# Twenty-four modulation vectors of layer 0 on the matrix engine, with the condition stationary and the weights moving

## The chip, the cores and the metric

The kernel runs on one core of one Trainium2 chip. TensorE (PE) multiplies matrices into eight PSUM banks, VectorE (DVE), ScalarE (ACT) and GpSimd (POOL) work on tiles in SBUF, and SyncE (SP) issues the DMAs. Each engine takes its instructions in a fixed order. The metric is the device time of one launch, in microseconds (us); the median of the runs counts.

## The reference, cut to what matters

One step of a hybrid diffusion backbone: two layers, 1024 latent and 128 context tokens, width 1024. Each layer begins with a modulation: from the condition `c` (and `c_ctx` for the context tokens) come six vectors of length 1024, which shift, scale and gate the stream.

```
mod = (jax.nn.silu(cvec) @ lp['w_mod'] + lp['b_mod'])[:, None, :]
sh1, sc1, g1, sh2, sc2, g2 = jnp.split(mod, 6, axis=-1)
h = x * (1 + sc1) + sh1
... = jnp.split(h @ lp['w_in'] + lp['b_in'], offsets, axis=-1)
mix = jnp.concatenate([a_out, m_out, g_out], axis=-1) @ lp['w_out']
x = layernorm(ALPHA * x + g1 * mix, lp['ln1_g'], lp['ln1_b'])
h2 = x * (1 + sc2) + sh2
```

`a_out` is latent attention, `m_out` an mLSTM, `g_out` an HGRN2 recurrence; they share the input projection. A SwiGLU feed-forward block follows, gated by `g2`.

## The kernel before

Per layer there are four phases: A (input projection, HGRN2, mLSTM, preparation of the attention's inputs), B (attention), C and D (output projection and feed-forward). Most products are made in three passes of reduced float32 (`mm3`, lines 155 to 157): each operand is split into a high and a low part, cast on ScalarE (L145, L150) and subtracted on POOL or DVE (L146, L151). `hhi` and `hlo` hold the two parts of the modulated stream. The HGRN2 and mLSTM products are plain float32.

The six modulation vectors of a layer are kept as 48 pieces of 128 values, `modfm[:, l, j, s]`, with j the piece and s one of the two conditions. Here "vector" means such a piece. In layer 0 pieces 0 to 15 are made in `start`, 16 to 23 in the background of the first projections, 24 to 39 in the background of the mLSTM, and 40 to 47 later. A background vector is a `mod_gemv`: one DMA of 128x1024 weights (L211), and for each of the two conditions one DVE instruction that multiplies the weights by the broadcast condition `cB` and sums along the row (L213). `mod_bias` (L220) adds the bias for eight at a time, and `gsave` (L225) writes the gate vectors to memory. Layer 1 makes none of its vectors in phase A; they are made in phase D of layer 0.

`start_mod` gives a generator. Each evacuation of the projection `gi` (L399) and of the attention's inputs takes one step of it, and each of the nine mLSTM blocks two.

Phase A in the order of the program, with the lines named later:

- `gi` projection (216 `mm3` products of 256 columns, evacuated by L399 on DVE), `prep`, and the projections for the attention
- HGRN2 for the first pair of heads: `states` (transposes L566, products L571), `outs` (products L601; POOL L614 to L617, ScalarE L618, DVE L619 to L623), with the projections of the second pair among them
- `ml_gates` (transposes L694, L741), then HGRN2 for the second pair, with `ml_states` (L781 to L807) and other projections among them
- `mlstm` for nine blocks: a broadcast load (L825), a mask on POOL (L832), exponentials on ScalarE (L835), products L830, L845 and L850 on PE, DVE L839 to L871, POOL L863 to L874
- `spill_gate` for `mo` and `gg`: 18 tiles of 24 `mm3` products with 256 columns, then DVE L336, ScalarE L337 (sigmoid or silu), POOL L338, and a store. In the program these come after `mlstm`.

Phase B begins with conversions of the attention's inputs. They are written into parts of `hhi` and `hlo`, which phase A's projections have read by then. The first score products and their maxima (L1134, L1135) lead to the first attention probabilities (L1183, L1184).

The PSUM banks are handed out from rings: `r_mm` is banks 0 to 2 (projections), `r_a` banks 3 and 4, `r_m` banks 5 to 7. A bank is written again only when its former content has been read, in the order of the program. Which ready instruction comes next on an engine is set when the program is built, by a list scheduler; an instruction whose inputs or whose bank aren't free yet is passed by later ones.

Of the kernel before, what the change touches and what calls it, by code (L numbers as in the profile page):

```python
# [15 lines left out]
BF16 = mybir.dt.bfloat16  # L16
AF = mybir.ActivationFunctionType
ALU = mybir.AluOpType
AX = mybir.AxisListType

P = 128
D = 1024
KD = 8
# [9 lines left out]
U = 1024  # L33
# [64 lines left out]
class Builder:  # L98
# [60 lines left out]
    def setup(self):  # L159
        nc, ctx, ins = self.nc, self.ctx, self.ins  # L160
# [3 lines left out]
        t = self.tile  # L164
# [5 lines left out]
        self.cols = t(self.pp, [P, DEPTH, NCOL], name="cols")  # L170
        nc.sync.dma_start(self.cols, ins["cols"])
        self.modfm = t(self.pp, [P, DEPTH, 48, 2], name="modfm")
        self.gates = t(self.pp, [P, NT, 16], name="gates")
        self.gT = t(self.pp, [16, P], name="gT")
        self.mhalf = t(self.pp, [P, 8], name="mhalf")
# [59 lines left out]
    def start(self, z):  # L235
        nc, ins = self.nc, self.ins
        accs = [(i // NB, i % NB, self.bank[i]) for i in range(7)]
        cin, cc = z([P, KD, 2]), z([P, KD, 2])
        cB, junk = [z([P, D]), z([P, D])], z([P, D], BF16)
        rm, rx, rt = z.ring(6, [P, U]), z.ring(6, [P, T]), z.ring(2, [P, T])  # L240
        nc.sync.dma_start(cin, ins["cvec"])
# [2 lines left out]
        xs, ws = [], []  # L244
# [35 lines left out]
        return ws, accs  # L280

    def start_mod(self, z, j0, j1):
        raw = z.ring(2, [P, U])
        cB, junk = [z([P, D]), z([P, D])], z([P, D], BF16)
        self.mod_init(cB)

        def gen():
            for j in range(j0, j1):
                self.mod_gemv(0, j, cB, raw.next(), junk)
                if j % 8 == 7:  # L290
                    self.mod_bias(0, j - 7, 8)
                if j == 23:
                    self.gsave(0, 16, self.r_m.next())
                yield

        return gen()
# [1393 lines left out]
def pack(i):  # L1690
# [7 lines left out]
    wm = f["w_mod"].reshape(DEPTH, KD, P, 48, P)  # L1698
    a["w_mod"] = np.concatenate([
        wm[0, :, :, :8].transpose(2, 3, 0, 1).reshape(8, P, 1024),  # L1700
        wm[0, :, :, 8:16].transpose(2, 1, 0, 3).reshape(8, P, 1024),
        wm[0, :, :, 16:].transpose(2, 3, 0, 1).reshape(32, P, 1024),
        wm[1].transpose(2, 3, 0, 1).reshape(48, P, 1024)], 0).reshape(DEPTH, 48, P, 1024)
    w = f["w_in"].reshape(DEPTH, KD, P, -1)
    units = np.zeros((DEPTH, 22, P, 1024), np.float32)
# [63 lines left out]
```

## Time and profile before

| | us |
|---|---|
| median of 3 runs | 3615.47 |
| lowest and highest | 3614.98, 3617.87 |
| the profiled execution | 3608.53 |
| its span | 3606.7 |
| PE busy | 3382.4 (94%) |
| DVE busy | 2251.9 (62%) |
| POOL busy | 1999.0 (55%) |
| ScalarE busy | 1635.2 (45%) |

The profiled execution is another one than the three timed runs. A row of the windows gives, for a stretch of time, how long each engine was busy in it and the clock that TensorE was granted (1.00 is 2.4 GHz, 0.50 is 1.2 GHz). A group by line gives the busy time of all instructions of one line, the mean of one, and how long the engine stood idle just before them and for whom. The timeline gives single instructions with their start; a matmul's duration overlaps the next one's start, so what one costs is read from start to start.

### The profile page before, as it was taken

The page shows a single profiled execution, that of the slowest core. Times are in us where ns is not written, and L with a number is a line of the kernel's source. Part 1 is how long each engine was busy: PE and PEld are TensorE (multiplying, and loading weights), DVE is VectorE, ACT ScalarE, POOL GpSimd, SP SyncE. Part 2 cuts the span into 40 slices and gives each one's busy share as a digit, 9 for nine tenths or more (in the row PEclk, how much of TensorE's full clock was granted, in tenths as well). Part 3 has the DMA queues.
Part 4 walks back from the last instruction along what each step waited for, and adds up shares of the span by engine and source line. Part 5 has one row for each costly group of instructions (what it writes and reads, how often), then busy time and mean ns, then how long its engine had stood idle before and what let it go on. Part 6 is the DMA issues. An engine that isn't in the chain of part 4 may idle for free. (4 is left out here: it accounts for less than half of the span.)

```text
span 3606.7 us, 56103 instructions
## 1 busy us (share of the span) xinstructions
PE 3382.4 (94%) x20556; PEld 3015.5 (84%) x20556; DVE 2251.9 (62%) x4487; ACT 1635.2 (45%) x2877; POOL 1999.0 (55%) x1750
## 2 busy tenths in 40 slices
PE   7998987998979999999889989989999899999989
PEld 7998876776779999988689888877767899999867
DVE  6878778556674444487776688765568544443344
ACT  4264654887343333312262646578863433333111
POOL 3465566877665555401454556457763555556345
PEclk9999976999989999999999999789999899999999
DMA  6211153002352222375422021401044322224232
GB/s 251 70 46 34 45 168 98 19 21 85 123 156 86 85 86 86 104 252 184 161 73 71 32 43 40 135 25 24 22 129 127 115 76 75 75 77 158 72 116 77
DMA packets 331274, 335.77 MB, mean 93 GB/s; under 512 B 191459, under 2 KB 270387, under 8 KB 330997
## 3 DMA queue, kind: packets, MB, share of 16 engines
q1 hardware_dynamic: 330996, 332.19, 29.3%
q8 instruction: 161, 2.64, 0.3%
q14 instruction: 117, 0.95, 0.1%
HBM read 263.54 MB, written 68.56 MB: 92 GB/s over the span
## 5 line engine op out<-in xcount | busy, mean ns | idle before, releaser
L151 POOL TENSOR_TENSOR t<-t,t 128x512 fp32r<-128x512 f32 (+3 forms) x318 | 440.5, 1387 | 384.9 <-ACT t L150 379.9
L1447 PE MATMUL bank<-hhi,t 128*128 128x256 f32 (+1 forms) x2816 | 571.2, 295 | 7.9 <-DVE t L1347 7.4
L150 ACT CAST t<-t 128x512 fp32r<-128x512 f32 (+5 forms) x404 | 270.5, 672 | 676.1 <-PE bank L1447 275.1
L155 PE MATMUL bank<-hhi,t 128*128 128x384 f32 (+1 forms) x1238 | 464.3, 381 | 24.8 <-ACT hhi L145 10.4
L157 PE MATMUL bank<-hhi,t 128*128 128x384 f32 (+1 forms) x1238 | 463.8, 376 | 5.8 <-DVE t L151 5.8
L156 PE MATMUL bank<-hlo,t 128*128 128x384 f32 (+1 forms) x1238 | 464.4, 375 | 4.6 <-POOL hlo L151 3.1
L1447 PEld LDWEIGHTS bank<-hhi,t 128*128 128x128 f32 x2816 | 456.4, 189 | 9.6 <-ACT t L150 7.4
L1185 POOL TENSOR_TENSOR t<-t,t 128x512 fp32r<-128x512 f32 (+1 forms) x304 | 384.2, 1283 | 123.4 <-ACT t L1184 107.4
L1447 PE MATMUL bank<-t,t 128*128 128x320 f32 (+1 forms) x3168 | 435.0, 297 | 4.6 <-ACT t L150 2.2
L1447 PEld LDWEIGHTS bank<-t,t 128*128 128x128 f32 x3168 | 428.2, 190 | 6.0 <-ACT t L150 3.0
L1447 PE MATMUL bank<-hlo,t 128*128 128x320 f32 (+1 forms) x1408 | 415.3, 295 | 0.1
L155 PE MATMUL bank<-t,hhi 128*128 128x256 f32 (+3 forms) x1232 | 387.1, 315 | 8.1 <-DVE t L1105 2.1
L156 PE MATMUL bank<-t,hhi 128*128 128x256 f32 (+3 forms) x1232 | 389.2, 316 | 4.9 <-POOL t L146 4.9
L157 PE MATMUL bank<-t,hlo 128*128 128x256 f32 (+3 forms) x1232 | 388.9, 316 | 0.1
L155 PEld LDWEIGHTS bank<-hhi,t 128*128 128x128 f32 x1238 | 241.4, 196 | 60.7 <-ACT hhi L145 11.3
L1135 DVE TENSOR_REDUCE t<-bank 128x1 f32<-128x384 f32 (+1 forms) x400 | 205.1, 539 | 129.9 <-PE bank L1134 127.5
L157 PEld LDWEIGHTS bank<-hhi,t 128*128 128x128 f32 x1238 | 240.9, 195 | 37.9 <-DVE t L151 9.0
L156 PEld LDWEIGHTS bank<-hlo,t 128*128 128x128 f32 x1238 | 241.3, 195 | 36.7 <-POOL hlo L151 3.9
L1447 PEld LDWEIGHTS bank<-hlo,t 128*128 128x128 f32 x1408 | 265.4, 189 | 0.4 <-issue 0.2
L213 DVE SCALAR_TENSOR_TENSOR t<-t,t 128x1024 bf16<-128x1024 f32 x176 | 239.4, 1360 | 36.0 <-DMA t<-in_w_mod_dram 29.0
L155 PEld LDWEIGHTS bank<-t,hhi 128*128 128x128 f32 x1232 | 240.4, 196 | 24.9 <-DVE t L1105 2.5
L156 PEld LDWEIGHTS bank<-t,hhi 128*128 128x128 f32 x1232 | 241.7, 196 | 21.1 <-POOL t L146 5.3
(355 smaller groups left out, 7250.6 us busy)
## 6 DMA issues: line engine op xcount, KB each, us to landing
t<-in_w_mod_dram SPq DMA_DIRECT2D x96, 512.0 KB
t<-in_w_ffn_in_dram SPq DMA_DIRECT2D x88, 512.0 KB
t<-in_w_ffn_out_dram SPq DMA_DIRECT2D x44, 512.0 KB
t<-in_w_in_dram SPq DMA_DIRECT2D x40, 512.0 KB
shid<-t SPq DMA_DIRECT2D x88, 160.0 KB
sx<-t SPq DMA_DIRECT2D x27, 512.0 KB
t<-sx SPq DMA_DIRECT2D x27, 512.0 KB
shid<-t SPq DMA_DIRECT2D x88, 128.0 KB
```

What stands on the lines that cost most here:

```text
L150: self.nc.scalar.copy(hi, src)
L151: (eng or self.nc.gpsimd).tensor_tensor(lo, src, hi.bitcast(F32), op=ALU.subtract)
L155: mm(ps, a[0], b[0], start=first, stop=False)
L156: mm(ps, a[0], b[1], start=False, stop=False)
L157: mm(ps, a[1], b[0], start=False, stop=last)
L213: nc.vector.scalar_tensor_tensor(junk, raw, 1.0, cB[s], op0=ALU.mult, op1=ALU.mult, accum_out=self.modfm[:, l, j, s:s + 1])
L1135: V.tensor_reduce(nm[:, i, b:b + 1] if i < 8 else nm[:, i, 3:4], ps, axis=AX.X, op=ALU.max, negate=True)
L1185: G.tensor_tensor(pl, e, ph.bitcast(F32), op=ALU.subtract)
L1447: mm(ps, a[x][:, k * P:(k + 1) * P], view(y, k, n0, n1), start=first and k == 0 and i == 0, stop=k == 3 and i == 2, skip_group_check=True)
```

## The change

`start_mod` makes four vectors at a time on PE. The weights of pieces 16 to 39 are laid out anew on the host, so that four loads hold 512 columns of the weight matrix for all 1024 rows. `cc`, the condition after silu, now stays in SBUF; it is the stationary operand with two columns. Eight plain float32 matmuls with 512 moving columns add up in one bank of `r_mm`, ScalarE copies the 2x512 result (L298 of the changed file), four small transposes turn it into columns (L301), and one DVE instruction adds the bias (L304). The broadcasts of the condition into `cB` for these vectors are gone, and so are 48 instructions of L213. A group takes three steps of the generator: one that issues the loads, an empty one, and one that computes.

```diff
--- before.py
+++ after.py
@@ -170,6 +170,7 @@
         self.cols = t(self.pp, [P, DEPTH, NCOL], name="cols")
         nc.sync.dma_start(self.cols, ins["cols"])
         self.modfm = t(self.pp, [P, DEPTH, 48, 2], name="modfm")
+        self.cc = t(self.pp, [P, KD, 2], name="cc")
         self.gates = t(self.pp, [P, NT, 16], name="gates")
         self.gT = t(self.pp, [16, P], name="gT")
         self.mhalf = t(self.pp, [P, 8], name="mhalf")
@@ -235,7 +236,7 @@
     def start(self, z):
         nc, ins = self.nc, self.ins
         accs = [(i // NB, i % NB, self.bank[i]) for i in range(7)]
-        cin, cc = z([P, KD, 2]), z([P, KD, 2])
+        cin, cc = z([P, KD, 2]), self.cc
         cB, junk = [z([P, D]), z([P, D])], z([P, D], BF16)
         rm, rx, rt = z.ring(6, [P, U]), z.ring(6, [P, T]), z.ring(2, [P, T])
         nc.sync.dma_start(cin, ins["cvec"])
@@ -280,16 +281,29 @@
         return ws, accs
 
     def start_mod(self, z, j0, j1):
-        raw = z.ring(2, [P, U])
-        cB, junk = [z([P, D]), z([P, D])], z([P, D], BF16)
-        self.mod_init(cB)
+        nc = self.nc
+        raw, row = z.ring(4, [P, U]), z.ring(1, [2, 512])
 
         def gen():
-            for j in range(j0, j1):
-                self.mod_gemv(0, j, cB, raw.next(), junk)
-                if j % 8 == 7:
-                    self.mod_bias(0, j - 7, 8)
-                if j == 23:
+            for j in range(j0, j1, 4):
+                ws = [raw.next() for _ in range(4)]
+                for u, w in enumerate(ws):
+                    nc.sync.dma_start(w, self.ins["w_mod"][0, j + u])
+                yield
+                yield
+                ps, r = self.r_mm.next(), row.next()
+                for k in range(KD):
+                    nc.tensor.matmul(ps[0:2, :], self.cc[:, k, :], ws[k // 2][:, (k % 2) * 512:(k % 2 + 1) * 512],
+                                     start=(k == 0), stop=(k == KD - 1))
+                nc.scalar.copy(r, ps[0:2, :])
+                ps = self.r_m.next()
+                for q in range(4):
+                    nc.tensor.transpose(ps[:, 2 * q:2 * q + 2], r[:, q * P:(q + 1) * P], self.ident[0:2, 0:2])
+                one = 1.0 if (j // 8) % 3 == 1 else 0.0
+                b = self.col(0, "bmod")[:, j:j + 4].unsqueeze(2).to_broadcast([P, 4, 2])
+                nc.vector.scalar_tensor_tensor(self.modfm[:, 0, j:j + 4, :], ps[:, 0:8].rearrange("p (j s) -> p j s", s=2), one, b,
+                                               op0=ALU.add, op1=ALU.add)
+                if j == 20:
                     self.gsave(0, 16, self.r_m.next())
                 yield
 
@@ -1699,7 +1713,8 @@
     a["w_mod"] = np.concatenate([
         wm[0, :, :, :8].transpose(2, 3, 0, 1).reshape(8, P, 1024),
         wm[0, :, :, 8:16].transpose(2, 1, 0, 3).reshape(8, P, 1024),
-        wm[0, :, :, 16:].transpose(2, 3, 0, 1).reshape(32, P, 1024),
+        wm[0, :, :, 16:40].reshape(4, 2, P, 6, 4, P).transpose(3, 0, 2, 1, 4, 5).reshape(24, P, 1024),
+        wm[0, :, :, 40:].transpose(2, 3, 0, 1).reshape(8, P, 1024),
         wm[1].transpose(2, 3, 0, 1).reshape(48, P, 1024)], 0).reshape(DEPTH, 48, P, 1024)
     w = f["w_in"].reshape(DEPTH, KD, P, -1)
     units = np.zeros((DEPTH, 22, P, 1024), np.float32)
```

The order of the instructions differs above all in four places. In the rows below `bank_63` to `bank_70` are banks 0 to 7; the changed file's lines are 14 higher than before from `start_mod` on.

TensorE, in the HGRN2 of the second pair of heads. Before (L601 and L571 are its products, L155 to L157 with 256 columns the spill's):

```order
L157 MATMUL bank_64<-t_134,hlo_77 128x256
L155 MATMUL bank_64<-t_134,hhi_76 128x256
L156 MATMUL bank_64<-t_138,hhi_76 128x256
L601 MATMUL bank_66<-t_1955,t_665 128x128
L571 MATMUL bank_70<-t_619,t_681 128x128 x2
L601 MATMUL bank_66<-t_1955,t_665 128x128
L601 MATMUL bank_67<-t_1955,t_665 128x128 x2
L601 MATMUL bank_66<-t_1955,t_665 128x128
L601 MATMUL bank_67<-t_1955,t_665 128x128
L571 MATMUL bank_69<-t_619,t_685 128x128 x2
L157 MATMUL bank_64<-t_134,hlo_77 128x256
L155 MATMUL bank_64<-t_134,hhi_76 128x256
```

After (L615, L585 and L580 are L601, L571 and L566 of before):

```order
L585 MATMUL bank_70<-t_615,t_681 128x128 x2
L580 MATMUL bank_68<-ident_71,t_623 128x128
L580 MATMUL bank_68<-ident_71,t_627 128x128
L580 MATMUL bank_70<-ident_71,t_623 128x128
L580 MATMUL bank_70<-ident_71,t_627 128x128
L585 MATMUL bank_69<-t_615,t_677 128x128 x2
L615 MATMUL bank_66<-t_665 128x128
L615 MATMUL bank_67<-t_665 128x128
L615 MATMUL bank_66<-t_665 128x128
L615 MATMUL bank_67<-t_665 128x128
L615 MATMUL bank_66<-t_665 128x128
L615 MATMUL bank_67<-t_665 128x128
```

The spill's products are gone from this place; 409 of them stood ahead of the first mLSTM product, and none does now.

TensorE, in the mLSTM. Before (L830, L845 and L850):

```order
L156 MATMUL bank_64<-t_138,hhi_76 128x256
L157 MATMUL bank_64<-t_134,hlo_77 128x256
L155 MATMUL bank_64<-t_134,hhi_76 128x256
L850 MATMUL bank_69<-t_611,t_4370 128x65
L845 MATMUL bank_70<-t_2986,t_4386 128x130 x2
L830 MATMUL bank_66<-t_4390,t_615 128x128 x2
L850 MATMUL bank_69<-t_611,t_4370 128x65 x3
L830 MATMUL bank_67<-t_4390,t_615 128x128 x2
L850 MATMUL bank_68<-t_611,t_4370 128x65 x4
L156 MATMUL bank_64<-t_138,hhi_76 128x256
```

After (L844, L859 and L864 are these lines; L296 is the new product):

```order
L859 MATMUL bank_69<-t_2991,t_4389 128x130 x2
L864 MATMUL bank_68<-t_607,t_4373 128x65 x3
L844 MATMUL bank_67<-t_4393,t_611 128x128 x2
L296 MATMUL bank_64<-t_4353,cc_81 2x512 x2
L864 MATMUL bank_70<-t_607,t_4373 128x65 x4
L296 MATMUL bank_64<-t_4357,cc_81 2x512
L864 MATMUL bank_69<-t_607,t_4377 128x65
L296 MATMUL bank_64<-t_4357,cc_81 2x512
L296 MATMUL bank_64<-t_4361,cc_81 2x512
L859 MATMUL bank_68<-t_2987,t_4393 128x130 x2
L864 MATMUL bank_69<-t_607,t_4377 128x65 x3
L296 MATMUL bank_64<-t_4361,cc_81 2x512
```

The new products stand among those of the first six blocks, 32 in all.

TensorE, at the last products of the mLSTM (L850, after the change L864). Before (L155 to L157 with 384 columns are phase B's first products):

```order
L845 MATMUL bank_68<-t_2986,t_4390 128x130 x2
L850 MATMUL bank_69<-t_611,t_4382 128x65 x4
L850 MATMUL bank_70<-t_611,t_4370 128x65 x4
L850 MATMUL bank_68<-t_611,t_4370 128x65 x4
L155 MATMUL bank_69<-hhi_76,t_5655 128x384
L156 MATMUL bank_69<-hlo_77,t_5655 128x384
L157 MATMUL bank_69<-hhi_76,t_5655 128x384
```

After:

```order
L155 MATMUL bank_63<-t_143,hhi_76 128x256
L156 MATMUL bank_63<-t_147,hhi_76 128x256
L864 MATMUL bank_68<-t_607,t_4373 128x65 x4
L157 MATMUL bank_63<-t_143,hlo_77 128x256
L155 MATMUL bank_63<-t_143,hhi_76 128x256
L156 MATMUL bank_63<-t_147,hhi_76 128x256
L157 MATMUL bank_63<-t_143,hlo_77 128x256
L155 MATMUL bank_64<-t_135,hhi_76 128x256
```

The products of phase B that followed here come later; in their place 388 of the spill's products stand in a row, and 44 among the mLSTM's last ones.

ScalarE, at the end of the spill. Before (L337 is the spill's, L835 the mLSTM's, L150 converts phase B's inputs):

```order
L337 ACT_TABLE_LOAD
L337 ACTIVATE t_162<-t_162 128x256
L150 CAST hhi_76<-t_5675 128x128
L835 ACT_TABLE_LOAD
L835 ACTIVATE t_4370<-t_4370,t_2802 128x128 x8
L150 CAST hhi_76<-t_5663 128x384
L150 CAST hhi_76<-t_5667 128x384
```

After (L351 is L337, L1059 is L1045 of before):

```order
L351 ACTIVATE t_163<-t_163 128x256
L351 ACTIVATE t_159<-t_159 128x256
L351 ACTIVATE t_163<-t_163 128x256
L1059 CAST t_5636<-t_5704 1x1152
L1059 CAST t_5728<-t_5704 1x1152
L1059 CAST hhi_76<-t_5704 1x1152
L150 CAST hhi_76<-t_5700 128x128
L150 CAST hhi_76<-t_5688 128x384
```

The conversions still stand behind the spill's last sigmoid, which now comes after the mLSTM's exponentials.

## Rows read from the trace of the kernel before

**Rows 1.** Page, part 1: engine, busy us, share of the span, instructions.

```profile
PE 3382.4 (94%) x20556; PEld 3015.5 (84%) x20556; DVE 2251.9 (62%) x4487; ACT 1635.2 (45%) x2877; POOL 1999.0 (55%) x1750
```

**Rows 2.** Windows: stretch, then PE, PEld, DVE, ACT, POOL busy; clock, DMA share, GB/s.

```profile
91.70:185.10 93.40, 88.08 (x702) 86.37 (x702) 80.99 (x245) 24.20 (x37) 46.08 (x46) 0.92 0.24 70
1900.80:1978.00 77.20, 77.20 (x674) 76.36 (x674) 46.59 (x192) 11.27 (x22) 29.47 (x33) 1.00 0.22 62
344.40:470.10 125.70, 120.07 (x929) 110.03 (x929) 94.77 (x249) 81.44 (x137) 75.38 (x111) 0.97 0.22 57
470.10:602.80 132.70, 95.58 (x429) 82.74 (x428) 117.61 (x321) 52.76 (x123) 93.97 (x94) 0.62 0.50 162
2143.60:2264.20 120.60, 115.10 (x907) 104.60 (x905) 98.45 (x256) 73.18 (x117) 75.59 (x106) 1.00 0.20 50
2264.20:2376.60 112.40, 94.92 (x450) 83.54 (x449) 90.92 (x287) 59.84 (x142) 55.22 (x65) 0.63 0.38 115
```

**Rows 3.** Lines L830, L1184 in layer 0: ns min/median/max, first to last start us.

```profile
L830 PE MATMUL bank<-t,t x72: 272/417/579, 470.1 to 533.3; 64*128 64x128 f32 x72
...
L1184 ACT CAST t<-t x152: 293/620/642, 602.8 to 914.5; 128x512 fp32r<-128x512 f32 x144, 128x128 fp32r<-128x128 f32 x8
```

**Rows 4.** Groups by line and form, DVE, 475 to 603 us: busy us, mean ns.

```profile
L213 DVE SCALAR_TENSOR_TENSOR t<-t,t 128x1024 bf16<-128x1024 f32 x32 | 42.7, 1334 | 1.8 <-DMA t<-in_w_mod_dram 1.8
L1135 DVE TENSOR_REDUCE t<-bank 128x1 f32<-128x384 f32 x19 | 9.6, 545 | 0.0
...
L213 DVE DVE_READ_ACCUMULATOR t<-t,t 128x1 f32 x32 | 2.5, 78 | 0.0
```

**Rows 5.** Timeline, PE, phase B: start us, us, line, operands, count.

```profile
653.91 0.40 PE L1181 MATMUL bank<-t,t 96*128 96x512 f32 x1
654.14 0.39 PE L1182 MATMUL bank<-t,t 97*128 97x512 f32 x1
```

**Rows 6.** Timeline, PE, first mLSTM products of layer 0.

```profile
476.35 0.71 PE L845 MATMUL bank<-t,t 128*128 128x130 f32 x4
476.99 0.71 PE L830 MATMUL bank<-t,t 64*128 64x128 f32 x4
477.63 0.88 PE L850 MATMUL bank<-t,t 128*128 128x65 f32 x6
478.44 0.71 PE L830 MATMUL bank<-t,t 64*128 64x128 f32 x4
```

**Rows 7.** Timeline, ScalarE and POOL, end of the spill in layer 0.

```profile
485.86 0.30 ACT L150 CAST hhi<-t 128x128 fp32r<-128x128 f32 x1
...
486.96 0.72 POOL L338 TENSOR_TENSOR t<-t,t 128x256 f32<-128x256 f32 x1
```

**Rows 8.** Windows of line L151 alone: DVE busy, POOL busy, clock, DMA.

```profile
487.00:603.00 116.00, 10.17 (x13) 21.46 (x16) 0.57 0.46 152
```

**Rows 9.** Timeline, PE, spill in layer 1: first and last of 38 rows.

```profile
2266.62 0.28 PE L156 MATMUL bank<-t,hhi 128*128 128x256 f32 x1
...
2270.81 0.28 PE L157 MATMUL bank<-t,hlo 128*128 128x256 f32 x1
```

**Rows 10.** Groups, DVE and POOL, 345 to 475 us: busy, mean ns, idle before.

```profile
L619 DVE TENSOR_TENSOR t<-t,t 128x192 f32<-128x192 f32 x18 | 7.9, 439 | 16.6 <-ACT t L618 16.6
L336 DVE TENSOR_TENSOR t<-bank,t 128x256 f32<-128x256 f32 x17 | 7.0, 413 | 3.5 <-DMA sgg<-t 3.5
...
L338 POOL TENSOR_TENSOR t<-t,t 128x256 f32<-128x256 f32 x17 | 12.6, 741 | 28.8 <-ACT t L337 28.1 <-DVE t L623 0.7
```

**Rows 11.** Timeline, PE, mLSTM of layer 1.

```profile
2284.75 1.97 PE L850 MATMUL bank<-t,t 128*128 128x65 f32 x8
2286.65 1.22 PE L830 MATMUL bank<-t,t 64*128 64x128 f32 x4
2287.80 0.69 PE L850 MATMUL bank<-t,t 128*128 128x65 f32 x2
```

**Rows 12.** Windows: 25 us of the mLSTM of layer 1.

```profile
2275.00:2300.00 25.00, 25.00 (x107) 22.72 (x107) 15.13 (x54) 22.55 (x58) 8.07 (x13) 0.50 0.57 180
```

## The prediction, made before the changed kernel was run

> **What bounds the kernel now.** I read the page first: TensorE (PE) is busy for 3382.4 us, 94% of the span [rows 1]. So the question is where PE is not the limit, and what the change does there. Next I cut the two layers' first phase into the same stretches and put them side by side [rows 2]. Layer 1 makes no modulation vectors in this phase, so it is a control for layer 0. Three stretches matter.
>
> Stretch A runs from the first evacuation of `gi` (L399) to the first state matmul (L571): 93.4 us in layer 0, 77.2 in layer 1 [rows 2]. In layer 1 PE is busy all the time; in layer 0 VectorE (DVE) also makes vectors 16 to 23 there. Stretch B runs from the last gate transposes (L741) to the first mLSTM product (L830): 125.7 us, PE busy 120.07. Stretch C runs from there to the first attention probabilities (L1184): 132.7 us, PE busy 95.58 at a granted clock of 0.62, DVE busy 117.61 [rows 2, 3]. C is the one stretch limited by DVE: vectors 24 to 39 cost it 32 x 1.334 = 42.7 us, and 2.5 us more for reading the accumulators [rows 4]. Layer 1 needs 112.4 us for C [rows 2]. So if the work simply vanished, the controls say some 16 us in A and 20 to 25 in B and C together (258.4 against 233.0).
>
> **What the change takes from DVE and puts on PE.** 48 of the products on DVE go, 48 x 1.334 = 64 us. In their place stand six groups of eight plain float32 matmuls with a 2-wide stationary operand and 512 moving columns. The trace counts two instructions for such a matmul, so 96. No row has a plain float32 matmul that wide. From below: reduced float32 with 512 columns starts every 0.233 us [rows 5]. From above: plain float32 with 130 columns and a full weight load starts every 0.16 us, (476.99 - 476.35) / 4, which scaled by columns is 0.63 [rows 6]. I take 0.43, the middle, since the narrow row also pays a load of 128 weight columns that a 2-wide operand doesn't need. A group then costs 16 x 0.43 = 6.9 us at full clock (3.7 to 10) and 13.8 at half. The Trainium skill, "FP8 and Floating Point Precision", TensorE Precision Notes, says that true FP32 takes four passes through the array; by it a matmul would take 4 x 512 / 2.4 GHz = 0.85 us as an estimate, and the six groups 41 us, the same sum; no run here shows the wide case. A 2x512 copy on ScalarE, four small transposes and one 128x8 add per group come to little on engines that are not the limit there.
>
> **Stretch A.** Two groups add 13.8 us to PE, and about 1 us for transposes and for the second group's weights, whose four loads wait for the first group. DVE loses 16 x 1.33 = 21 us. Layer 1 shows this stretch to be bound by PE as soon as DVE is free: 77.2 + 13.8 + 1 = 92, against 93.4. I take -1 us (-7 to +5, by the bounds of a group). DVE's relief is spent on PE's new work.
>
> **What moves: the spill matmuls.** This is the term that decides. The 432 matmuls of `spill_gate` (mo, gg; 128x256) come after `mlstm` in the program and use banks 0 to 2. Before, nothing in `mlstm` used these banks, so 409 of the 432 stand on PE ahead of the first L830, between the hgrn products. The new groups take banks from the same ring, so the spill now has to come after the last group: the order shows none of it in B, 44 among the last mLSTM products, and 388 in one piece behind the last one. And the conversions for phase B write into `hhi` and `hlo`, which the spill reads. Before, the spill's last gate product ran on POOL at 486.96 us and the first conversion on ScalarE at 485.86 [rows 7], so all of this conversion, 21.46 us of L151 on POOL and 10.17 on DVE [rows 8], lay beside the mLSTM. Now it starts when the 388 are done.
>
> Stretch B loses 409 x 0.113 = 46 us of PE work (38 rows, 2266.62 to 2270.81, so 0.113 each) [rows 9], but DVE then sets the pace: 94.77 us busy, less 7.0 for the spill's L336, gives 88. It waited 16.6 us there for ScalarE, and POOL 28.8 us in front of L338 [rows 2, 10]; both shrink when the spill's sigmoids no longer stand between the hgrn's steps. At 95% busy that is 93 us, at the 82% of layer 1's row (98.45 of 120.60) 107 [rows 2]. I take 100, the middle, a gain of 26.
>
> Stretch C falls into three pieces in a row. First the mLSTM with four groups. At full clock its own 72 + 64 + 144 instructions take 0.16, 0.16 and 0.135 us each [rows 6], 41 us; four groups 27.5; 44 spill matmuls 5: 73 in all. At half clock they take 0.29 and 0.24, (2287.80 - 2286.65) / 4 and (2286.65 - 2284.75) / 8 [rows 11], and with 0.29 for the 64 as well that is 74 us; groups 55, spill 5: 134. Which clock? In layer 1 PE is busy 25.00 of 25 us here at a clock of 0.50 [rows 12], so its own products don't raise it; the wide ones are unlike them. The weights also need time: 16 x 0.52 MB and 9 broadcasts of 0.52 MB are 13 MB, 81 us at the 162 GB/s of this stretch [rows 2], and the first loads of the weights stand behind four broadcasts. I take 95, between 73 and 134 and nearer to the first, since the wide products fill PE's columns as the spill's do. Second the 388 spill matmuls at 0.113 us: 44. Third the conversions and the first peaks: 21.5 on POOL [rows 8], then 19 reductions on DVE, 9.6 [rows 4], are 31 if all else hides under them; with an estimate of 8 for the casts ahead and the products between 39, and I take that (31 to 42). It was hidden under the mLSTM and the vectors before.
>
> The sum for B and C: 100 + 95 + 44 + 39 = 278, against 258.4, so +19.6; with A +19 us. From L1184 on the attention is bound by PE as before, and nothing is late that would absorb it. One load of weights is also moved up in SP's queue into the start, but a broadcast of the same size goes from there: nothing. The profiled execution took 3608.5 us (span 3606.7 and 1.8 around it), 7.0 below the median of 3615.5. So 3627 by that execution, and **3634.5 us** by the median.
>
> **Rival 1, faster.** The wide matmuls bring PE to full clock through the mLSTM and the weights arrive in time. Then 93 + 73 + 44 + 31 = 241, -17 us, with A -18: 3597. For it: the spill's products kept the clock at 0.97 in B [rows 2], and DVE has 45 us less to do. Against it: the serial order of mLSTM, spill and conversions remains, and with the likely B and third piece the first piece must stay under 75 us for any gain. The Trainium skill, "Perfetto Trace Analysis", Matmul Optimizations, says that the engine scales with utilization, so that matmuls should come back to back in batches; by that this rival would be the likely one, but the row of layer 1, back to back at half clock, disagrees [rows 12].
>
> **Rival 2, much slower.** PE stays at half clock through all four groups, or waits in them for weights, which in its queue also holds up the mLSTM products behind. Then 107 + 134 + 44 + 42 = 327, +69, with A +68: 3683. It decides once the first piece of C is over 115 us. The row of layer 1 speaks for it.
>
> **Rival 3, no change.** B is at 93 and the first piece near 82, and the gain in B pays for what is laid bare in C: within 7 us of 3615.5.
>
> **How the numbers follow.** My forecast, +8 to +40 us, has 0.42; rival 2 and all over +40, 0.20; rival 1, 0.22; rival 3, 0.16. Slower by over 0.2% (7 us, about what a measurement of this kernel can tell from none): 0.62; within: 0.16; faster: 0.22. The likeliest case alone spans 3623 to 3655. The range 3602 to 3670 leaves out the far half of rival 1 and the far end of rival 2, some 0.2 together.
>
> **What would show it.** Right: in the windows of the profile after, a stretch of some 44 us with nothing on PE but 128x256 matmuls at full clock after the last mLSTM product, DVE low in it, and the first `hhi` conversion right behind; B near 100 us; A within 5 us of 93. Wrong: 512-column matmuls far from 0.43 us at clock 1.00; a clock near 1.00 through the mLSTM (rival 1); PE waiting for `in_w_mod` there (rival 2); or spill matmuls that wait for something other than their bank. If B didn't shrink, the loss would be some 26 us larger.

## The result, and the profile after

The changed kernel takes 3639.11 us (median of 4 runs, 3631.05 to 3641.91) against 3615.22 for the kernel before on the same chip: 1.0064 times the time, 95% interval 1.0044 to 1.0085. It is slower by some 24 us. The profiled execution took 3640.93 us, with a span of 3639.1, 32.4 above that of before; the stretches below add up to this larger difference. In the code after, lines from L297 of before on are 14 higher: L399 is L413, L571 is L585, L830 is L844, L1184 is L1198.

The page of the kernel after, engines over the whole span, answers to [rows 1]:

```profile
PE 3430.1 (94%) x20676; PEld 3029.1 (83%) x20676; DVE 2190.2 (60%) x4394; ACT 1602.7 (44%) x2854; POOL 1972.0 (54%) x1750
```

DVE is relieved by 61.7 us, PE has 47.7 us more, and the share of PE is what it was. The page alone explains nothing; the stretches do. Windows of the kernel after (columns as in [rows 2]): stretch A, stretch B, the three pieces of C, and C as a whole.

```profile
86.10:188.40 102.30, 97.20 (x714) 84.24 (x713) 60.66 (x218) 25.33 (x40) 37.62 (x42) 0.97 0.24 69
...
350.60:460.60 110.00, 87.58 (x512) 76.41 (x512) 89.95 (x230) 37.76 (x93) 63.57 (x95) 0.70 0.17 40
460.60:543.80 83.20, 83.20 (x414) 50.11 (x414) 40.06 (x177) 19.49 (x59) 37.71 (x59) 0.89 0.51 167
543.80:592.00 48.20, 46.47 (x388) 46.26 (x386) 13.68 (x47) 11.30 (x23) 24.70 (x33) 1.00 0.29 89
592.00:640.40 48.40, 33.45 (x128) 28.77 (x129) 31.52 (x62) 30.95 (x63) 20.79 (x21) 0.64 0.33 102
460.60:640.40 179.80, 163.12 (x927) 125.14 (x927) 85.26 (x284) 61.73 (x144) 83.20 (x111) 0.85 0.40 129
```

Against [rows 2]: A is 8.9 us longer, but begins 5.6 earlier, so its end is 3.3 late. B is 15.7 us shorter, C 47.1 longer. The fourth row is the serial run of the spill: 388 matmuls at clock 1.00, and DVE busy 13.68 of 48.20. The fifth is what had lain beside the mLSTM before. The next stretch (A to B) loses 2.9 us more, and the attention of layer 0 wins 5.4 back. Together that is 3.3 + 2.9 - 15.7 + 47.1 - 5.4 = 32.2 of the 32.4 us.

How the run of spill products ends and the conversions begin: timeline of the kernel after, the last spill product on PE and the product behind it, then ScalarE (start us, us, line).

```profile
589.99 0.28 PE L157 MATMUL bank<-t,hlo 128*128 128x256 f32 x1
598.39 0.69 PE L155 MATMUL bank<-hhi,t 128*128 128x384 f32 x1 [8.12 <-ACT t L150]
```

```profile
591.36 2.20 ACT L1059 CAST t<-t 1x1152 fp32r<-1x1152 f32 x2
593.47 1.14 ACT L1059 CAST hhi<-t 1x1152 fp32r<-1x1152 f32 x1
594.64 1.12 ACT L150 CAST hhi<-t 128x128 fp32r<-128x128 f32 x3
```

The first cast into `hhi` starts at 593.47 us, 3.5 us after the start of the last spill product, and PE stands 8.12 us. Before, conversions ran from 485.86 us on [rows 7].

### The profile page after: what moved, and what is told of

Same layout as the page of the kernel before. It is cut to its first block, busy times and chain, and to the rows that moved or that the text cites. A ratio compares the mean times of both kernels' runs of the same rounds, so it can differ in the third digit from the quotient of the medians.

```text
span 3639.1 us, 56221 instructions
## 1 busy us (share of the span) xinstructions
PE 3430.1 (94%) x20676; PEld 3029.1 (83%) x20676; DVE 2190.2 (60%) x4394; ACT 1602.7 (44%) x2854; POOL 1972.0 (54%) x1750
## 5 line engine op out<-in xcount | busy, mean ns | idle before, releaser
L151 POOL TENSOR_TENSOR t<-t,t 128x512 fp32r<-128x512 f32 (+4 forms) x318 | 440.1, 1385 | 396.4 <-ACT t L150 391.9
L150 ACT CAST t<-t 128x512 fp32r<-128x512 f32 (+6 forms) x404 | 270.3, 672 | 660.8 <-PE bank L1461 281.5
L155 PE MATMUL bank<-hhi,t 128*128 128x384 f32 (+1 forms) x1238 | 461.2, 380 | 33.2 <-ACT t L150 14.3
L157 PE MATMUL bank<-hhi,t 128*128 128x384 f32 (+1 forms) x1238 | 462.9, 375 | 5.4 <-DVE t L151 5.3
L155 PE MATMUL bank<-t,hhi 128*128 128x256 f32 (+3 forms) x1232 | 383.1, 312 | 5.1 <-ACT t L513 2.0
L157 PE MATMUL bank<-t,hlo 128*128 128x256 f32 (+3 forms) x1232 | 385.6, 314 | 0.1
L155 PEld LDWEIGHTS bank<-hhi,t 128*128 128x128 f32 x1238 | 241.7, 196 | 68.3 <-ACT t L150 15.2
L157 PEld LDWEIGHTS bank<-hhi,t 128*128 128x128 f32 x1238 | 241.1, 195 | 35.6 <-DVE t L151 8.4
L155 PEld LDWEIGHTS bank<-t,hhi 128*128 128x128 f32 x1232 | 237.6, 194 | 23.0 <-ACT t L513 2.2
L157 PEld LDWEIGHTS bank<-t,hlo 128*128 128x128 f32 x1232 | 238.6, 194 | 14.8 <-POOL hlo L151 0.6
## 6 DMA issues: line engine op xcount, KB each, us to landing
shid<-t SPq DMA_DIRECT2D x88, 128.0 KB
```

What stands on the lines that cost most here:

```text
L150: self.nc.scalar.copy(hi, src)
L151: (eng or self.nc.gpsimd).tensor_tensor(lo, src, hi.bitcast(F32), op=ALU.subtract)
L155: mm(ps, a[0], b[0], start=first, stop=False)
L157: mm(ps, a[1], b[0], start=False, stop=last)
```

## The experiments

I cut every run into the same stretches. Times are us; "A ends" is the first start of the line of L571, B + C the time from the first L741 to the first L1184, each by its number in that kernel.

| kernel | A | A ends | B | C | B + C | median | ratio to before, 95% interval |
|---|---|---|---|---|---|---|---|
| before | 93.4 | 185.1 | 125.7 | 132.7 | 258.4 | 3615 | 1 |
| after | 102.3 | 188.4 | 110.0 | 179.8 | 289.8 | 3639.11 | 1.0064 (1.0044 to 1.0085) |
| e1_ring | 102.2 | 188.2 | 128.1 | 113.4 | 241.5 | 3601.56 | 0.9958 (0.9945 to 0.9972) |
| e2_spill_late | 93.7 | 189.6 | 106.6 | 175.6 | 282.2 | 3639.72 | 1.0065 (1.0052 to 1.0079) |
| e3_double | 101.7 | 187.2 | 108.7 | 204.3 | 313.0 | 3676.69 | 1.0171 (1.0154 to 1.0188) |
| e4_copy_dve | 98.0 | 183.2 | 107.2 | 177.3 | 284.5 | 3634.23 | 1.0050 (1.0035 to 1.0065) |
| e5_ring_copy | 100.6 | 188.0 | 128.0 | 118.9 | 246.9 | 3602.27 | 0.9962 (0.9949 to 0.9976) |
| e6_second_only | 94.4 | 186.0 | 125.6 | 110.2 | 235.8 | 3588.22 | 0.9923 (0.9907 to 0.9940) |
| e7_no_vectors | 79.3 | 164.7 | 132.0 | 105.4 | 237.4 | 3577.80 | 0.9894 (0.9878 to 0.9910) |
| e8_fill | 102.0 | 187.6 | 113.8 | 172.8 | 286.6 | 3646.70 | 1.0087 (1.0074 to 1.0100) |
| e9_first_only | 101.8 | 187.4 | 125.4 | 139.7 | 265.1 | 3614.70 | 1.0001 (0.9991 to 1.0012) |
| e10_all_late | 80.4 | 164.9 | 137.7 | 124.0 | 261.7 | 3593.13 | 0.9941 (0.9927 to 0.9954) |
| e11_spill_early | 101.6 | 186.6 | 146.5 | 112.9 | 259.4 | 3641.66 | 1.0075 (1.0058 to 1.0093) |
| e12_spill_after_o2 | 102.1 | 187.7 | 130.7 | 109.6 | 240.3 | 3597.96 | 0.9950 (0.9932 to 0.9967) |

My theory: the loss is the place of the spill. The wide products take banks of the spill's ring, so the spill runs after the mLSTM, and the conversions, which write where the spill reads, after that. The rival: the 41 us of added matrix work are the price, on an engine that is busy 94% of the span.

### The ring alone, undone (e1_ring)

```diff
-                ps, r = self.r_mm.next(), row.next()
+                ps, r = (self.r_mm if j < 24 else self.r_m).next(), row.next()
```

> The changed kernel with one edit: the wide products of vectors 24 to 39 (beside the mLSTM) take their bank from the ring of banks 5 to 7 instead of the ring of banks 0 to 2, which the spill uses. The work is the same to the last instruction; in program order on TensorE 409 of the 432 spill products stand ahead of the first mLSTM product again (0 in the changed kernel). My theory (the shared ring puts the spill, and behind it the conversions, into a serial tail): stretch B goes back to about 125 us, the 46 us spill run and the bare conversions vanish from C, and C is 112 to 122 us against 179.8 changed and 132.7 before; the loss left is the 3 us that stretch A gives at its end. Time 3600 to 3610, ratio to before 0.996 to 0.999. Rival a (41 us of new work on an engine that is busy 94% of the span is the price, wherever it stands): 3632 to 3642 as the changed kernel. Rival b (the order matters, but the mLSTM then waits for its own banks, which the wide products now share): C 135 to 150, 3620 to 3632.

Windows of e1_ring, B and C:

```profile
350.40:478.50 128.10, 122.63 (x929) 112.38 (x929) 95.28 (x250) 81.78 (x139) 75.16 (x111) 0.96 0.22 56
478.50:591.90 113.40, 98.75 (x507) 67.05 (x506) 77.54 (x258) 54.62 (x126) 71.25 (x95) 0.88 0.56 179
```

The same work with another bank takes 3601.56 us, 37.6 below the changed kernel and faster than before. B is back at 128, and C is 66 us shorter than in the changed kernel and 19 shorter than before. The rival that counts PE's work falls.

### The spill late, without the new work (e2_spill_late)

On the kernel before, in `tm_group` and `spill_gate`:

```diff
-            ps = self.r_mm.next()
+            ps = (ring or self.r_mm).next()
...
-        self.win_tm(l, name, evac)
+        self.win_tm(l, name, evac, self.r_m if l == 0 else None)
```

> The kernel before with one edit: in layer 0 the 432 spill products take banks 5 to 7, which the mLSTM also uses, so that all of them stand behind the mLSTM; no vector is moved off VectorE. My theory: the place of the spill alone loses time. Stretch B shrinks from 125.7 to about 110 us, C grows from 132.7 to some 180 to 190 (mLSTM limited by VectorE some 85, spill 46 to 52, conversions and first peaks 50): net +30 to +45, 3645 to 3660. Rival a (the new matrix work is the price): B and C trade evenly, 3610 to 3622.

```profile
349.70:456.30 106.60, 85.54 (x513) 74.30 (x513) 91.72 (x230) 36.06 (x86) 63.72 (x95) 0.74 0.18 42
456.30:631.90 175.60, 152.95 (x848) 139.61 (x847) 122.37 (x346) 60.95 (x146) 98.47 (x112) 0.70 0.44 137
```

Not one vector is moved off DVE, and the kernel is slower by as much as the changed one: B + C is 282.2 against 258.4, +23.8, and the median 22.8 above before. My +30 to +45 was too high, mostly in C, but the sign and the shape are those of the theory. So the place of the spill costs some 23 us by itself. The two halves don't simply add up, though. With the spill late, moving the vectors is worth nothing (3639.72 with them on DVE, 3639.11 with them on PE): the mLSTM's piece of C took 72 us here (456.3 to 528.7) and 83.2 with the wide products in it. With the spill early, moving them pays (e1_ring).

### The price of the wide products (e3_double)

```diff
-                for k in range(KD):
+                for k in list(range(KD)) * (2 if j >= 24 else 1):
```

> The changed kernel with the wide products of vectors 24 to 39 done twice (64 more instructions of 2x512, the first pass overwritten by the second, same result). Measures the price of the wide products where they stand. If the stretch ahead of the spill is bound by TensorE throughout, as its 83.2 us busy of 83.2 say: 64 x 0.435 = +28 us over the changed kernel, 3664 to 3670. Rival (their weights, 81 us of transfers, or ScalarE and VectorE set that stretch and TensorE's busy time there is stretched by waiting): under +12 us, 3640 to 3651.

PE by line (busy us, mean ns of one), the wide products of the kernel after from 340 to 650 us:

```profile
L296 PE MATMUL bank<-t,cc 128*2 128x512 f32 x64 | 33.0, 643 | 0.0
```

and those of e3_double from 455 to 600 us:

```profile
L296 PE MATMUL bank<-t,cc 128*2 128x512 f32 x128 | 59.1, 603 | 0.0
```

The time is above my 3664 to 3670. The 64 extra instructions add 26.1 us of busy PE, 0.41 us each, and 24.5 us to C, as the theory wanted. The stretch was bound by PE, as its 83.20 of 83.20 said. By the profiles the first L1198 comes 22.2 us later and the end 36.0; the 14 us between arise where the two programs are alike (the attention of layer 1 took 313.6 us against 307.7, for one). What causes them stays open. It sets a limit to all readings here: that same stretch took 305.4 us in the trace of before and 314.7 in that of e2_spill_late, so a few us in a single trace decide nothing.

### What stretch A costs (e4_copy_dve, e5_ring_copy, e6_second_only, e9_first_only)

PE's small transposes wait for the copy on ScalarE. Timeline of the kernel after in stretch A, first PE, then ScalarE:

```profile
86.61 7.03 PE L296 MATMUL bank<-t,cc 128*2 128x512 f32 x16
93.57 0.48 PE L615 MATMUL bank<-t,t 64*128 64x128 f32 x2
...
102.34 0.58 PE L301 MATMUL bank<-ident,t 2*128 2x2 f32 x4 [5.10 <-ACT t L298]
```

```profile
95.75 1.28 ACT L546 ACT_TABLE_LOAD   x1
...
97.59 1.28 ACT L573 ACT_TABLE_LOAD   x1
...
101.30 0.52 ACT L573 ACTIVATE t<-t 128x384 f32<-128x384 f32 x1 [1.37 <-POOL t L572]
101.72 0.56 ACT L298 COPY t<-bank 2x512 f32<-2x512 f32 x1
```

The wide products end at 93.6 us, but ScalarE copies their result only at 101.72, behind `prep`'s activations. It stood still for only 2.1 us of the time between, 1.37 of them for POOL; the rest are the activations and two loads of their tables, 1.28 us each. PE stood 5.10 us. So I put the copy on DVE:

```diff
-                nc.scalar.copy(r, ps[0:2, :])
+                (nc.vector.tensor_copy if j < 24 else nc.scalar.copy)(r, ps[0:2, :])
```

> The changed kernel with the 2x512 copy of vectors 16 to 23 on VectorE instead of ScalarE. In stretch A the small transposes waited 5.1 us for that copy, which stood behind prep's activations in ScalarE's order, and 2 to 3 us more in the second group. If that wait is why stretch A cost +8.7 us and not -1: stretch A 93 to 97 us instead of 102.1, time 4 to 8 us below the changed kernel, 3631 to 3636. Rival (it only moves the wait to VectorE's order, or stretch A is limited by the added matrix work): 100 to 104 us, and 3637 to 3642.

A took 98.0 us and its end came 5 us earlier, but PE still waited, now 3.1 us for DVE (who waited for whom on PE, e4_copy_dve, 85 to 184 us: in total, times, longest):

```profile
PE bank L301 <- DVE t L298: 3.1, 1, 3.1
```

The time fell by 5 us, inside the two intervals. With the ring of e1_ring as well:

> Both edits that helped so far together: the wide products of vectors 24 to 39 on banks 5 to 7 (as e1_ring) and the 2x512 copy of vectors 16 to 23 on VectorE (as e4_copy_dve). They touch stretches that lie apart. My theory: they add up, stretch A near 98 us and C near 113, so 4 to 6 us below e1_ring: 3594 to 3599, ratio to before 0.994 to 0.9955. Rival (what A gains is lost again where the mLSTM begins, for its weights arrive no earlier): as e1_ring, 3600 to 3604.

A ended at 188.0, as in e1_ring, and the time was the same as there (3602.27), which is what the rival said. The gain of e4_copy_dve did not come again, so the engine of the copy settles nothing. More telling is to leave one half of the change out. Only vectors 24 to 39 on PE, on banks 5 to 7:

```diff
-                        bg = self.start_mod(Zone(self, c, "gemv"), 16, 24) if l == 0 else iter(())
+                        bg = self.start_mod_v(Zone(self, c, "gemv"), 16, 24) if l == 0 else iter(())
```

(`start_mod_v` is `start_mod` of the kernel before; the weights of pieces 16 to 23 keep their old layout.)

> Only vectors 24 to 39 (beside the mLSTM) go to the matrix engine, on banks 5 to 7; vectors 16 to 23 stay on VectorE as before the change. It tells what the part in stretch A is worth. My theory: in A the exchange is even (VectorE was the limit before, TensorE would be after), so A and the start stay as before (185 us at its end), C as in e1_ring (113 us): 3597 to 3602, the same as e1_ring within its interval or 1 to 4 us better, for e1_ring's A ended 3 us late. Rival (the part in A carries some of the gain of e1_ring): 3605 to 3612.

This is the fastest version that computes everything: 3588.22 us, 0.9923 of before, and 9 us below the range I gave. Its windows of A and C, and its timeline on PE in C:

```profile
91.60:186.00 94.40, 89.56 (x703) 87.84 (x702) 81.14 (x245) 24.38 (x37) 46.26 (x46) 0.92 0.24 71
...
472.10:582.30 110.20, 96.97 (x503) 63.17 (x502) 76.28 (x253) 54.29 (x125) 72.36 (x95) 0.91 0.57 183
```

```profile
497.63 1.11 PE L880 MATMUL bank<-t,t 128*128 128x65 f32 x8
498.54 0.42 PE L155 MATMUL bank<-hhi,t 128*128 128x384 f32 x1
...
503.49 6.30 PE L296 MATMUL bank<-t,cc 128*2 128x512 f32 x12
509.72 0.44 PE L155 MATMUL bank<-hhi,t 128*128 128x384 f32 x1
...
543.11 0.34 PE L156 MATMUL bank<-hlo,t 128*128 128x384 f32 x1
```

The first products of phase B (384 columns, from `hhi`) run at 498.54 us between mLSTM products (L880) and wide ones. In the changed kernel the first of them came at 598.39 us. Nothing is in line here: the mLSTM, the vectors and the conversions go at the same time. The other half alone, vectors 16 to 23 on PE as in the changed kernel:

> The other half of the change alone: vectors 16 to 23 on the matrix engine as in the changed kernel (banks 0 to 2, copy on ScalarE), vectors 24 to 39 on VectorE as before; 409 spill products ahead of the mLSTM as before. By the stretches of e1_ring and e6_second_only: A 102 us with its end 2 to 3 us later than before, B and C as before (126 and 133). Theory (only the late end of A is lost): 3616 to 3621, ratio 1.000 to 1.0015. Rival (the 13 us by which e6_second_only is below e1_ring are all the price of this half): 3624 to 3632, ratio 1.0025 to 1.0045.

3614.70 us, no difference from before, and a little under my 3616 to 3621. But C took 139.7 us where I expected 133, and in its trace the first L1184 starts 12.1 us later than before (614.9 against 602.8) while the whole span is only 2.6 longer: the rest came back in stretches that are alike. In A, PE is busy 96.68 us against 88.08, DVE 60.48 against 80.99:

```profile
85.60:187.40 101.80, 96.68 (x713) 83.73 (x712) 60.48 (x218) 25.28 (x40) 37.49 (x42) 0.97 0.24 69
```

So by the medians the first half is worth nothing, and the second half, on its own banks, is worth 27 us. If the two added up, both together would give about 0.992, but e1_ring gave 0.9958, 13 us more than e6_second_only. The two traces lie 23.7 us apart in their spans: e6_second_only starts the last L1184 of layer 0 9.0 us before e1_ring (893.0 against 902.0), and the other 14.7 lie behind it, in stretches that are alike. What they are stays open.

### The bounds: no vectors, and all of them late (e7_no_vectors, e10_all_late)

> The kernel before without vectors 16 to 39 of layer 0: their loads, products and bias are left out (a constant stands in their place). It bounds what any way of making them could give. From the control of layer 1: A 77 to 82 us instead of 93.4, B 125 as before, C 105 to 114 instead of 132.7; time 3575 to 3590. Theory: e1_ring has got most of that in C (113) and nothing in A. Rival (C is limited by something else than VectorE, the transfers or the clock): C above 120, time 3595 to 3605.

```profile
85.40:164.70 79.30, 77.50 (x661) 76.07 (x662) 58.52 (x212) 22.87 (x36) 36.17 (x40) 1.00 0.22 62
...
459.90:565.30 105.40, 91.97 (x431) 79.20 (x430) 78.09 (x249) 56.78 (x138) 75.66 (x100) 0.68 0.40 122
```

With the rest of the program as it is, all that any way of making these vectors could give is 37 us (0.9894). e6_second_only has 27 of them. A is 14 us shorter than before and C 27; B, where I expected 125 us, took 132.0 and lost 6 of them. To get those of A, all 24 vectors went beside the mLSTM:

```diff
-                        bg = self.start_mod(Zone(self, c, "gemv"), 16, 24) if l == 0 else iter(())
+                        bg = iter(())
...
-                bg = self.start_mod(zl, 24, 40) if l == 0 else iter(())
+                bg = self.start_mod(zl, 16, 40) if l == 0 else iter(())
```

(and the wide products on banks 5 to 7.)

> All 24 vectors beside the mLSTM on the matrix engine, banks 5 to 7; none in stretch A (six groups in C instead of four). By e7_no_vectors A falls to about 79 us and its end to 165; C had TensorE busy 97.0 of 110.2 us with four groups (e6_second_only), two more are 13.9 us, of which at most the 13 idle ones can be hidden. Theory (TensorE sets C as soon as it has this work): A -15 against e6_second_only, C 115 to 124, 3577 to 3586. Rival (the work is not hidden at all and B loses what A gains, as in e7_no_vectors, where it took 132.0): 3586 to 3594, as e6_second_only.

```profile
331.00:468.70 137.70, 127.35 (x942) 116.31 (x942) 102.95 (x252) 82.85 (x143) 82.99 (x116) 0.95 0.23 56
468.70:592.70 124.00, 113.10 (x553) 68.02 (x552) 80.20 (x265) 53.35 (x125) 70.61 (x95) 0.92 0.61 194
```

A fell to 80.4 us as expected, C rose to the top of what I gave, and B took 137.7 us: the rival. A ended 21.1 us earlier than in e6_second_only (14 of it its length, the rest its start), but of that 5.6 went in the stretch between and 12.1 in B, so that C began only 3.4 earlier. 3593.13 us is no better than e6_second_only.

### Is the clock what B lacked? (e8_fill)

In `outs`, ahead of each pair of products, layer 0, second pair of heads:

```diff
+                if l == 0 and p == 1:
+                    for ps in pair:
+                        for i in range(3):
+                            nc.tensor.matmul(ps[:, :BW], self.hhi[:, i, 0:P], self.hhi[:, i, 0:BW], start=(i == 0), stop=(i == 2))
```

> The changed kernel with idle work on TensorE in stretch B: ahead of each of the 21 pairs of hgrn products of the second head pair in layer 0 stand six 128x384 products whose result is overwritten, 126 instructions of about 0.16 us, some 20 us. Stretch B took 110.0 us where I had predicted 100, at a granted clock of 0.70 where the kernel before had 0.97 with the spill in it, and the mean of the 240 hgrn products was 394 ns against 293. Theory (the missing 10 us are the clock, which falls when the spill no longer fills TensorE): with the fill the clock of B is above 0.9, the products come back to about 300 ns, and B takes 100 to 107 us in spite of the added work; time 3629 to 3637. Rival (the chain over GpSimd, ScalarE and VectorE sets B and the clock doesn't matter, or the fill delays the products): B 111 to 128, time 3640 to 3657.

PE by line, 345 to 470 us, the hgrn products of the kernel after:

```profile
L615 PE MATMUL bank<-t 64*128 64x128 f32 x228 | 33.6, 392 | 16.1 <-DVE t L635 12.4 <-DVE t L637 2.3 <-ACT t L657 1.5
```

and of e8_fill, with the fill itself, then its window of B:

```profile
L614 PE MATMUL bank<-hhi 128*128 128x384 f32 x129 | 34.1, 381 | 4.7 <-DVE t L641 4.7
L619 PE MATMUL bank<-t 64*128 64x128 f32 x240 | 33.3, 305 | 3.9 <-DVE t L639 3.9
```

```profile
349.40:463.20 113.80, 104.35 (x665) 88.90 (x664) 91.33 (x228) 35.93 (x84) 67.86 (x99) 0.93 0.16 37
```

The clock rose from 0.70 to 0.93 and a product fell from 392 to 305 ns, as the theory wanted, and B still took 113.8 us, as the rival said. But the rival names two reasons, and this run doesn't tell them apart. The 126 fill products of B had PE busy for 32.9 us where I had given them some 20, and six of them stand ahead of each pair of products that DVE waits for. DVE's waits for the hgrn products in B grew with it (who waited for whom on DVE in B, first the kernel after, then e8_fill: in total, times, longest):

```profile
DVE t L637 <- PE bank L615: 7.4, 9, 1.8
```

```profile
DVE t L641 <- PE bank L619: 12.1, 13, 2.6
```

So the fill may have taken back what the clock gave. Whether the low clock sets B, or a chain from POOL over ScalarE and DVE back to PE, stays open.

### The order of the program instead of the ring (e11_spill_early, e12_spill_after_o2)

```diff
-                order = "0 1 2 p s o0 3 4 o1 5 o2"
+                order = "0 1 2 p s o0 3 4 o1 5 6 7 o2"
```

(6 and 7 are the two calls that make the spill, o2 the last hgrn outputs.)

> The changed kernel with all banks as they are, and the two calls that make the spill written ahead of the last hgrn outputs, so before the mLSTM in the program: all 432 spill products stand ahead of the first mLSTM product though the ring is shared. It undoes the serial tail by another lever than e1_ring. My theory (order alone is the cause): B 126 to 133, C 105 to 116, 3597 to 3609. Rival (sharing banks 0 to 2 with the wide products itself makes the mLSTM or the conversions wait): C over 125 and 3615 to 3630.

```profile
348.30:494.80 146.50, 122.14 (x945) 113.42 (x945) 110.36 (x264) 80.44 (x150) 88.25 (x122) 0.88 0.24 66
494.80:607.70 112.90, 104.34 (x491) 69.82 (x491) 70.53 (x246) 40.14 (x103) 60.41 (x84) 0.80 0.50 159
```

I missed by 33 us. C came out as the theory said (112.9), but my edit did two more things: the spill now went ahead of the last hgrn outputs, and it did so in layer 1 too. The last products of the hgrn then stood bare, at half clock and waiting (timeline of e11_spill_early, PE):

```profile
478.83 1.65 PE L615 MATMUL bank<-t 64*128 64x128 f32 x12 [8.07 <-DVE t L635]
483.30 2.21 PE L615 MATMUL bank<-t 64*128 64x128 f32 x12 [2.81 <-DVE t L637]
```

B of layer 1 took 146.9 us for 120.6 before. I read it as the same mechanism on the other side: whatever the spill doesn't cover lies bare. Without this, in layer 0 alone and behind the hgrn outputs:

```diff
-                order = "0 1 2 p s o0 3 4 o1 5 o2"
+                order = "0 1 2 p s o0 3 4 o1 5 o2" + (" 6 7" if l == 0 else "")
```

> The edit of e11_spill_early without its side effect, and in layer 0 alone: all banks as in the changed kernel, the two calls that make the spill written behind the last hgrn outputs and ahead of the mLSTM. All 432 spill products stand ahead of the first mLSTM product, and no hgrn product stands behind the last of them (32 did in e11_spill_early, whose stretch B took 146.5 us in layer 0 and 146.9 in layer 1, where 120.6 was usual). My theory (the place of the spill, not the bank itself, decides): B 126 to 132, C 108 to 117, attention from about 595, 3597 to 3609. Rival (something in e11_spill_early other than the bare hgrn outputs costs, or the shared banks do): 3615 to 3642.

```profile
349.80:480.50 130.70, 125.40 (x950) 115.23 (x950) 95.46 (x251) 84.59 (x144) 75.82 (x112) 0.96 0.22 59
480.50:590.10 109.60, 94.14 (x485) 59.43 (x484) 75.98 (x259) 52.08 (x120) 70.98 (x95) 0.93 0.57 181
```

3597.96 us, with all banks as in the changed kernel. So not the bank itself costs, but the order that sharing it forces.

## Why the prediction was right, point by point

**The direction and the cause: right.** I forecast 3634.5 us (3602 to 3670) and the kernel took 3639.11. The term that I said decides, the spill behind the mLSTM and the conversions behind the spill, is shown from three sides: undone by the ring (e1_ring) and by the order (e12_spill_after_o2) it turns the loss into a gain of 15 to 18 us, and done alone (e2_spill_late) it costs 23. The run of 388 with the conversions behind it is there as forecast. Two of the signs I had named failed: A is 102.3 us and not within 5 of 93, and B is 110 and not near 100.

**The sum came close in part by luck.** Its errors cancel only in part: the first piece of C was 12 us shorter than I said, but B was 10 longer and the third piece 11. By the profiled executions, from which all terms come, I forecast 3627 us and it took 3640.93, 14 more. That the median is only 4.6 off is chance: the profiled execution of before was 7 below its median, and that of after 1.8 above its own. The pieces, predicted and measured:

| term | predicted | measured |
|---|---|---|
| A | -1 (-7 to +5) | +8.9 in length, +3.3 at its end |
| B | 100 (93 to 107) | 110.0 |
| C, mLSTM and four groups | 95 (73 to 134) | 83.2 |
| C, spill run | 44 | 46, of which 388 at 0.12 |
| C, conversions and first peaks | 39 (31 to 42) | 50.4 |
| C | 178 | 179.8 |
| B + C | 278 | 289.8 |

*A.* The failed step is "a 2x512 copy on ScalarE [...] come to little on engines that are not the limit there". ScalarE had time in A as a whole (busy 25.33 of 102.30 us), but none at this place: the copy stood behind `prep`'s activations and their table loads, and PE waited 5.10 us. From e7_no_vectors A takes 79.3 us without vectors; two groups are 13.9 and the wait 5.1; of the 4 us left some 2 lie right behind the wait, where the clock was 0.50 and the products started every 0.21 us, not every 0.12, until 107.3; the rest has no row of its own. The window behind the wait:

```profile
102.30:105.00 2.70, 2.66 (x14) 2.65 (x15) 0.17 (x1) 0.52 (x1) 2.63 (x3) 0.50 0.02 6
```

DVE's relief did appear, but at the start of A, which came 5.6 us earlier; there I had put nothing. The attention behind C, for which I had also put nothing, gave 5.4 us back.

*B.* The lower end was set by DVE 95% busy, the upper by the 82% of layer 1's row, and I took the middle. DVE was busy 89.95 of 110.00, 82%: the row of layer 1 was the one to take. Whether the clock of 0.70 had a part in it e8_fill doesn't settle.

*The wide products.* 0.43 us was right to a per cent: 16 of them from 86.61 to 93.57 us, 0.435 each. The Trainium skill, "FP8 and Floating Point Precision", TensorE Precision Notes, counts four passes for true FP32, which gave the estimate of 0.85 us for a matmul of two instructions; the trace agrees with 0.87. At half clock one took 0.88, (474.12 - 470.61) / 4:

```profile
470.61 3.57 PE L296 MATMUL bank<-t,cc 128*2 128x512 f32 x4
474.12 1.97 PE L864 MATMUL bank<-t,t 128*128 128x65 f32 x8
```

*The first piece.* The clock was 0.89, half only until the first wide products were through, so it took 83.2 and not 95. Windows of 10 us, ahead of the first wide product and among them:

```profile
460.60:470.60 10.00, 10.00 (x39) 8.63 (x38) 5.43 (x24) 3.36 (x13) 2.55 (x3) 0.50 0.63 214
...
480.00:490.00 10.00, 10.00 (x48) 4.42 (x47) 4.88 (x21) 3.02 (x9) 4.21 (x7) 1.00 0.59 199
```

On the clock rival 1 was nearer than I. My reason, that the wide products fill PE's columns as the spill's do, no run tests; the rows show only that the clock rose among them.

*The third piece.* I took the work of POOL for the limit (21.5 us) and hid the rest under it. Laid bare, PE waited 8.1 us for the first casts, of which 3.3 went to three casts of a single row that stood first on ScalarE (591.36 to 594.64) and 1.5 to a load of weights that one cast waited for; then PE ran at a clock of 0.64 and waited eight times more, 8.6 us. No engine was busy for more than 33.5 of the 48.4 us, so I take the chain through all of them for the limit. No run tests that by itself.

**The rivals.** Rival 2 (half clock through the groups) fell: 83.2 us, not 115. Rival 1 had the serial order in its sum too (44 and 31) and failed by the sizes: B was 110 and not 93, the first piece 83.2 and not 73, the third 50.4 and not 31. That e12_spill_after_o2 (3597.96) and e1_ring (3601.56) come near its 3597 is chance, for in them B is long and the serial pieces are gone. The Trainium skill's rule in "Perfetto Trace Analysis", Matmul Optimizations, that the engine scales its power with utilization, so that matmuls should come back to back, would have favoured it. The trace agrees where the wide products stand: C ran at 0.68 without vectors (e7_no_vectors), at 0.91 with four groups in it (e6_second_only). It disagrees for the mLSTM's own products, which had PE busy 25.00 of 25 us at 0.50 [rows 12]. My trust in that one row was too broad; it speaks of narrow products only.

## What to carry to other kernels

Moving work off the engine that limits a stretch can be worth what that stretch shows, here 27 of 37 us, but only if the new work takes nothing that other work needs to run beside it. A bank from a shared ring is such a thing: the order of the program decides who gets it first, and one more user in the wrong place put 388 matmuls and all conversions behind it into one line. Before costing the operations, look for what else takes from the same ring, and when; and where work is made bare, don't price it by its busiest engine alone: the third piece took 50 us where the busiest engine had some 33.

## What the runs showed of the hardware that I had not expected

PE was busy without a gap at half clock in the first rows of the mLSTM (10.00 of 10 us at 0.50), and just as busy at full clock once the wide products, plain float32 with a two-column stationary operand and 512 moving columns, stood among the others (10.00 of 10 us at 1.00). Without any wide products the clock was still at half, with PE as busy, later in the mLSTM (e7_no_vectors):

```profile
500.00:510.00 10.00, 10.00 (x40) 8.87 (x39) 8.95 (x27) 4.47 (x14) 9.84 (x14) 0.50 0.36 107
```

Over all of C the clock was 0.68 without them, and 0.91 and 0.92 with four and six groups (e6_second_only, e10_all_late). What it is in these products that goes with the rise, no run tells. The four groups are 28 us of work at full clock, yet C took 110.2 us with them and 105.4 without, and B and C together 235.8 and 237.4.

Filling TensorE with idle work brought its clock from 0.70 to 0.93 in B (e8_fill), and B took 113.8 us in place of 110.0.
